# Rotary embedding, fp32: from bf16 passes on ScalarE and VectorE to fp32 in place in a ring, with GpSimd and VectorE computing

## The chip, the cores and the metric

One core of one Trainium2 chip. The metric is the device time of one execution in microseconds (us), median of several executions. "Span" is the time from the first to the last recorded instruction or transfer of the profiled execution; here a time is its span plus 1.7 to 2.2 us. All runs below were in the fast state, with a granted clock of 1.0.

## The reference, cut to what matters

```python
x: [16, 512, 1024] fp32;  cos, sin: [512, 32] fp32;  16 heads of 64
x1, x2 = x[..., :32], x[..., 32:]              # halves of each head
out = concat([x1*cos - x2*sin, x1*sin + x2*cos], axis=-1)   # fp32, [16, 512, 16, 64]
```

The kernel reads 33.5 MB and writes 33.5 MB and does six operations per pair of elements. In the kernel before, the transfers occupy the DMA engines for 98% of the span (below).

## The kernel before

A tile is one batch entry: 4 rows of DRAM (16 KB) to each of 128 partitions, 2 MB. The last two tiles are split into halves and quarters. ScalarE converts a tile to bf16, VectorE does four bf16 operations, ScalarE converts the result back to fp32 and issues the store.

```python
# SyncE: loads, three buffers deep
sp.wait_ge(sem_ci, t - NX + 1)
sp.dma_start(x_sb[:, xb, 0:E], x_tile_ap(t)).then_inc(sem_in[xb], 16)
# ... cut: tables, loaded behind the first tile ...
# ScalarE
ae.activation(xb_sb[:, cb, 0:E], x_sb[:, xb, 0:E], ACT_COPY)          # fp32 -> bf16
ae.activation(o_sb[:, ob, 0:Eu], ob_sb[:, obb, 0:Eu], ACT_COPY)       # bf16 -> fp32
ae.dma_start(out_tile_ap(u), o_sb[:, ob, 0:Eu])
# VectorE, all bf16
ve.tensor_tensor(t1v, xbv, cos_b, mult)
ve.tensor_tensor(t2v, xbv, sin_b, mult)
ve.tensor_tensor(obv[:, :, 0:HALF], t1[:, :, 0:HALF], t2[:, :, HALF:HD], subtract)
ve.tensor_tensor(obv[:, :, HALF:HD], t2[:, :, 0:HALF], t1[:, :, HALF:HD], add)
```

Of the kernel before, what the change touches and what calls it, by code (L numbers as in the profile page):

```python
# [1 line left out]

# [4 lines left out]
def bass_split_heads_rope_kernel(  # L8
    nc: bass.Bass,
    x: bass.AP,  # L10
    cos: bass.AP,
    sin: bass.AP,
    num_heads: bass.AP,
    out: bass.AP,
):
    batch, seq, dim = x.shape
    H = int(num_heads)
    HD = dim // H
    HALF = HD // 2
    P = 128  # L20
    assert seq % P == 0
    SPP = seq // P

    tiles = [(b, 0, SPP) for b in range(batch)]

    def _split(tile, parts):
        b, j0, nj = tile
        if nj % parts != 0:
            return [tile]
        q = nj // parts  # L30
        return [(b, j0 + i * q, q) for i in range(parts)]

    if len(tiles) >= 2:
        t_last = tiles.pop()
        t_prev = tiles.pop()
        tiles += _split(t_prev, 2) + _split(t_last, 4)
    NT = len(tiles)

    ROWS = SPP * H
    RE = ROWS * HD  # L40

    NX = 3
    NC = 3
    NO = 3
    NOB = 3
    NTMP = 2

    fp32 = mybir.dt.float32
    bf16 = mybir.dt.bfloat16
    mult = mybir.AluOpType.mult  # L50
    add = mybir.AluOpType.add
    subtract = mybir.AluOpType.subtract
    ACT_COPY = mybir.ActivationFunctionType.Copy

    with ExitStack() as stack:  # L55
        cos_sb = stack.enter_context(nc.sbuf_tensor([P, SPP, HALF], fp32))
        sin_sb = stack.enter_context(nc.sbuf_tensor([P, SPP, HALF], fp32))
        coscat_sb = stack.enter_context(nc.sbuf_tensor([P, SPP, HD], bf16))
        sincat_sb = stack.enter_context(nc.sbuf_tensor([P, SPP, HD], bf16))
        x_sb = stack.enter_context(nc.sbuf_tensor([P, NX, RE], fp32))  # L60
        xb_sb = stack.enter_context(nc.sbuf_tensor([P, NC, RE], bf16))
        o_sb = stack.enter_context(nc.sbuf_tensor([P, NO, RE], fp32))
        ob_sb = stack.enter_context(nc.sbuf_tensor([P, NOB, RE], bf16))
        tmp1_sb = stack.enter_context(nc.sbuf_tensor([P, NTMP, ROWS, HD], bf16))
        tmp2_sb = stack.enter_context(nc.sbuf_tensor([P, NTMP, ROWS, HD], bf16))
        sem_tab = stack.enter_context(nc.semaphore("sem_tab"))
        sem_tab2 = stack.enter_context(nc.semaphore("sem_tab2"))
        sem_in = [stack.enter_context(nc.semaphore(f"sem_in{i}")) for i in range(NX)]
        sem_out = [stack.enter_context(nc.semaphore(f"sem_out{i}")) for i in range(NO)]
        sem_ci = stack.enter_context(nc.semaphore("sem_ci"))  # L70
        sem_co = stack.enter_context(nc.semaphore("sem_co"))
        sem_vp = stack.enter_context(nc.semaphore("sem_vp"))
        sem_vf = stack.enter_context(nc.semaphore("sem_vf"))
        block = stack.enter_context(nc.Block(no_gpsimd_drain=False))

        cos_v = cos.rearrange("(p j) d -> p (j d)", p=P)
        sin_v = sin.rearrange("(p j) d -> p (j d)", p=P)

        def x_tile_ap(t):
            b, j0, nj = tiles[t]  # L80
            v = x[b, :, :].rearrange("(p j) d -> p j d", p=P)
            return v[:, j0:j0 + nj, :].rearrange("p j d -> p (j d)")

        def out_tile_ap(t):
            b, j0, nj = tiles[t]
            v = out[b, :, :, :].rearrange("(p j) h d -> p j (h d)", p=P)
            return v[:, j0:j0 + nj, :].rearrange("p j e -> p (j e)")

        def uses(nbuf, b):
            return (NT - b + nbuf - 1) // nbuf  # L90

        @block.sync
        def _(sp):
            for t in range(NT):
                xb = t % NX
                _, _, nj = tiles[t]
                E = nj * H * HD
                if t >= NX:
                    sp.wait_ge(sem_ci, t - NX + 1)
                sp.dma_start(x_sb[:, xb, 0:E], x_tile_ap(t)).then_inc(sem_in[xb], 16)  # L100
                if t == 0:
                    sp.dma_start(  # L102
                        cos_sb[:].rearrange("p j d -> p (j d)"), cos_v
                    ).then_inc(sem_tab, 16)
                    sp.dma_start(
                        sin_sb[:].rearrange("p j d -> p (j d)"), sin_v
                    ).then_inc(sem_tab, 16)

        @block.scalar
        def _(ae):  # L110
            ae.wait_ge(sem_tab, 32)
            last = ae.activation(coscat_sb[:, :, 0:HALF], cos_sb[:, :, :], ACT_COPY)  # L112
            last = ae.activation(coscat_sb[:, :, HALF:HD], cos_sb[:, :, :], ACT_COPY)  # L113
            last = ae.activation(sincat_sb[:, :, 0:HALF], sin_sb[:, :, :], ACT_COPY)  # L114
            last = ae.activation(sincat_sb[:, :, HALF:HD], sin_sb[:, :, :], ACT_COPY)  # L115
            last.then_inc(sem_tab2, 1)

            LEAD = 2
            for it in range(NT + LEAD):
                u = it - LEAD  # L120
                if u >= 0:
                    ob = u % NO
                    obb = u % NOB
                    _, _, nju = tiles[u]
                    Eu = nju * H * HD
                    ae.wait_ge(sem_vf, u + 1)
                    if u >= NO:
                        ae.wait_ge(sem_out[ob], 16 * (u // NO))
                    ae.activation(  # L129
                        o_sb[:, ob, 0:Eu], ob_sb[:, obb, 0:Eu], ACT_COPY  # L130
                    ).then_inc(sem_co, 1)
                    ae.wait_ge(sem_co, u + 1)
                    ae.dma_start(out_tile_ap(u), o_sb[:, ob, 0:Eu]).then_inc(sem_out[ob], 16)  # L133
                t = it
                if t < NT:
                    xb = t % NX
                    cb = t % NC
                    _, _, nj = tiles[t]
                    E = nj * H * HD
                    ae.wait_ge(sem_in[xb], 16 * (t // NX + 1))  # L140
                    if t >= NC:
                        ae.wait_ge(sem_vp, t - NC + 1)
                    ae.activation(  # L143
                        xb_sb[:, cb, 0:E], x_sb[:, xb, 0:E], ACT_COPY
                    ).then_inc(sem_ci, 1)
            for b in range(NO):
                ae.wait_ge(sem_out[b], 16 * uses(NO, b))

        @block.vector
        def _(ve):  # L150
            for t in range(NT):
                bt, j0, nj = tiles[t]
                R = nj * H
                E = R * HD
                cb = t % NC
                tb = t % NTMP
                obb = t % NOB
                if t == 0:
                    ve.wait_ge(sem_tab2, 1)
                ve.wait_ge(sem_ci, t + 1)  # L160
                if t >= NTMP:
                    ve.wait_ge(sem_vf, t - NTMP + 1)
                xbv = xb_sb[:, cb, 0:E].rearrange("p (j h d) -> p j h d", j=nj, h=H)
                t1 = tmp1_sb[:, tb, 0:R, :]
                t2 = tmp2_sb[:, tb, 0:R, :]
                t1v = t1.rearrange("p (j h) d -> p j h d", j=nj)
                t2v = t2.rearrange("p (j h) d -> p j h d", j=nj)
                cos_b = coscat_sb[:, j0:j0 + nj, None, :].broadcast_to([P, nj, H, HD])
                sin_b = sincat_sb[:, j0:j0 + nj, None, :].broadcast_to([P, nj, H, HD])
                ve.tensor_tensor(t1v, xbv, cos_b, mult)  # L170
                ve.tensor_tensor(t2v, xbv, sin_b, mult).then_inc(sem_vp, 1)  # L171
                ve.wait_ge(sem_vp, t + 1)
                if t >= NOB:
                    ve.wait_ge(sem_co, t - NOB + 1)
                obv = ob_sb[:, obb, 0:E].rearrange("p (r d) -> p r d", d=HD)
                ve.tensor_tensor(  # L176
                    obv[:, :, 0:HALF], t1[:, :, 0:HALF], t2[:, :, HALF:HD], subtract
                )
                ve.tensor_tensor(  # L179
                    obv[:, :, HALF:HD], t2[:, :, 0:HALF], t1[:, :, HALF:HD], add  # L180
                ).then_inc(sem_vf, 1)


# [1 line left out]
_INS = ['x', 'cos', 'sin', 'num_heads']  # L185
_OUTS = [((16, 512, 16, 64), 'float32')]
#: Inputs that are plain numbers.
_NUMBERS = {'num_heads': 16}


# [24 lines left out]
```

## Time and profile before

163.83 us (median of 3, 163.76 to 163.84), span 162.1 us.

The page of the kernel before, parts 1 to 5, cut. In part 1 a number is busy time, its share of the span, and the count of instructions. In part 2 each digit is the busy share of one fortieth of the span, in tenths. In part 5 the first pair of numbers is total busy us and mean ns of one instruction, and after the bar stands the idle time in front of them, with what ended it. DVE is VectorE, ACT is ScalarE, POOL is GpSimd; a q after a name stands for that engine's sequencer, which issues and waits. The last line is a group of DMA issues, with the size of each and the median us from issue to landing.

```profile
span 162.1 us, 266 instructions
DVE 111.3 (69%) x80; ACT 118.6 (73%) x45; POOL 0.2 (0%) x4
DMA  5999999999999999999999999999999999999985
q1 hardware_dynamic: 3168, 33.69, 49.5%
q10 hardware_dynamic: 2880, 33.56, 48.6%
...
DMA 54%; ACT 30%; issue 7%; DVE 5%; ACTq 1%; SPq 0%; DVEq 0%
...
L143 ACT ACTIVATE xb_sb<-x_sb 128x4096 bf16<-128x4096 f32 (+2 forms) x20 | 58.7, 2933 | 19.9 <-DMA x_sb<-in_x_dram 17.1
L170 DVE TENSOR_TENSOR tmp_sb<-xb_sb,coscat_sb 128x4096 bf16<-128x4096 bf16 (+2 forms) x20 | 37.3, 1865 | 45.8 <-ACT xb_sb L143 45.8
...
out_dram<-o_sb ACTq DMA_DIRECT2D x4, 512.0 KB, 3.6
```

The two transfer queues (q1 loads, q10 stores) occupy the 16 DMA engines for 98% of the span, and the row of 9s has no hole. The compute engines have a quarter to spare. The table by windows gives the same with numbers; its columns are the stretch and its length, busy time and count of VectorE, ScalarE and GpSimd, the TensorE clock, the DMA share and GB/s.

```profile
20.00:40.00 20.00, 18.27 (x11) 18.18 (x6) 0.00 (x0) 1.00 1.01 425
120.00:140.00 20.00, 14.37 (x13) 15.95 (x6) 0.00 (x0) 1.00 1.02 432
155.00:158.00 3.00, 2.05 (x4) 1.84 (x3) 0.00 (x0) 1.00 0.85 345
158.00:160.00 2.00, 0.00 (x0) 0.91 (x1) 0.00 (x0) 1.00 0.54 217
160.00:162.10 2.10, 0.00 (x0) 0.00 (x0) 0.00 (x0) 1.00 0.50 205
```

So 425 to 432 GB/s is what the transfers reach in this kernel when nothing holds them up, and only the ends lose time.

### The profile page before, as it was taken

To read this page: it belongs to the slowest core of one execution; us is meant where nothing else is said; L and a number is where in the kernel's file an instruction comes from. 1 tells how busy PE (TensorE), PEld (TensorE's weight loads), DVE (VectorE), ACT (ScalarE), POOL (GpSimd) and SP (SyncE) were. 2 spreads that over 40 slices of the span, in tenths; PEclk is the share of its full clock that TensorE was granted. 3 is DMA by queue.
4 is the path that set the end of the run, shared out by engine and by line. 5 is a ranking of instruction groups with operands and counts; after the bars stand their busy time and mean duration, and the time that the engine had idled before them with its cause. 6 is when DMAs were issued, how large, how long until landed. Compare 5 with 4: busy or idle time off the path is not lost.

```text
span 162.1 us, 266 instructions
## 1 busy us (share of the span) xinstructions
DVE 111.3 (69%) x80; ACT 118.6 (73%) x45; POOL 0.2 (0%) x4
## 2 busy tenths in 40 slices
DVE  0006997989898989896939488492966994635450
ACT  3078389898989898967588775868859787445552
POOL 0000000000000000000000000000000000000000
DMA  5999999999999999999999999999999999999985
GB/s 158 417 429 449 421 421 412 429 437 421 437 437 425 433 437 421 437 437 425 433 437 417 441 437 414 441 437 417 441 417 427 437 421 444 436 409 423 426 360 212
DMA packets 6050, 67.26 MB, mean 415 GB/s; under 512 B 672, under 2 KB 928, under 8 KB 1952
## 3 DMA queue, kind: packets, MB, share of 16 engines
q1 hardware_dynamic: 3168, 33.69, 49.5%
q10 hardware_dynamic: 2880, 33.56, 48.6%
q14 instruction: 2, 0.02, 0.0%
HBM read 33.69 MB, written 33.55 MB: 415 GB/s over the span
## 4 chain that ended last, share of the span: by engine, by line
DMA 54%; ACT 30%; issue 7%; DVE 5%; ACTq 1%; SPq 0%; DVEq 0%
DMA x_sb<-in_x_dram 49%; ACT xb_sb L143 15%; ACT o_sb L129 14%; DMA sin_sb<-in_sin_dram 5%; DVE tmp_sb L171 2%; DVE tmp_sb L170 1%; ACTq L133 1%; DVE ob_sb L176 1%; DVE ob_sb L179 1%; SPq L102 0%; SPq L100 0%; DVEq L55 0%; ACT coscat_sb L112 0%; ACT sincat_sb L115 0%; ACT coscat_sb L113 0%
## 5 line engine op out<-in xcount | busy, mean ns | idle before, releaser
L143 ACT ACTIVATE xb_sb<-x_sb 128x4096 bf16<-128x4096 f32 (+2 forms) x20 | 58.7, 2933 | 19.9 <-DMA x_sb<-in_x_dram 17.1
L170 DVE TENSOR_TENSOR tmp_sb<-xb_sb,coscat_sb 128x4096 bf16<-128x4096 bf16 (+2 forms) x20 | 37.3, 1865 | 45.8 <-ACT xb_sb L143 45.8
L129 ACT ACTIVATE o_sb<-ob_sb 128x4096 f32<-128x4096 bf16 (+2 forms) x20 | 58.6, 2929 | 12.7 <-DMA out_dram<-o_sb 7.5
L171 DVE TENSOR_TENSOR tmp_sb<-xb_sb,sincat_sb 128x4096 bf16<-128x4096 bf16 (+2 forms) x20 | 37.1, 1857 | 0.0
L176 DVE TENSOR_TENSOR ob_sb<-tmp_sb 128x2048 bf16<-128x2048 bf16 (+2 forms) x20 | 20.2, 1011 | 0.7
L179 DVE TENSOR_TENSOR ob_sb<-tmp_sb 128x2048 bf16<-128x2048 bf16 (+2 forms) x20 | 20.1, 1004 | 0.0
L112 ACT ACTIVATE coscat_sb<-cos_sb 128x128 bf16<-128x128 f32 x1 | 0.3, 309 | 7.0 <-DMA sin_sb<-in_sin_dram 7.0
L112 ACT ACT_TABLE_LOAD x1 | 1.3, 1283 | 0.7 <-PEq L197 0.7
L113 ACT ACTIVATE coscat_sb<-cos_sb 128x128 bf16<-128x128 f32 x1 | 0.3, 293 | 0.0
L115 ACT ACTIVATE sincat_sb<-sin_sb 128x128 bf16<-128x128 f32 x1 | 0.3, 293 | 0.0
L114 ACT ACTIVATE sincat_sb<-sin_sb 128x128 bf16<-128x128 f32 x1 | 0.3, 292 | 0.0
L197 POOL MEMSET const-bfloat16-1.0<- 128x1 bf16 x1 | 0.1, 101 | 0.0
L197 POOL MEMSET const-uint8-127<- 128x1 uint8 x1 | 0.1, 101 | 0.0
L197 POOL MEMSET const-float32-0.0<- 128x1 f32 x1 | 0.1, 98 | 0.2 <-issue 0.2
L197 POOL MEMSET const-float32-1.0<- 128x1 f32 x1 | 0.1, 98 | 0.0
## 6 DMA issues: line engine op xcount, KB each, us to landing
x_sb<-in_x_dram SPq DMA_DIRECT2D x14, 2048.0 KB, 16.8
out_dram<-o_sb ACTq DMA_DIRECT2D x14, 2048.0 KB, 19.7
x_sb<-in_x_dram SPq DMA_DIRECT2D x2, 1024.0 KB, 21.9
x_sb<-in_x_dram SPq DMA_DIRECT2D x4, 512.0 KB, 16.0
out_dram<-o_sb ACTq DMA_DIRECT2D x2, 1024.0 KB, 12.4
out_dram<-o_sb ACTq DMA_DIRECT2D x4, 512.0 KB, 3.6
cos_sb<-in_cos_dram SPq DMA_DIRECT2D x1, 64.0 KB, 7.3
sin_sb<-in_sin_dram SPq DMA_DIRECT2D x1, 64.0 KB, 7.3
```

The costliest lines, as they stand in the source:

```text
L112: last = ae.activation(coscat_sb[:, :, 0:HALF], cos_sb[:, :, :], ACT_COPY)
L113: last = ae.activation(coscat_sb[:, :, HALF:HD], cos_sb[:, :, :], ACT_COPY)
L114: last = ae.activation(sincat_sb[:, :, 0:HALF], sin_sb[:, :, :], ACT_COPY)
L115: last = ae.activation(sincat_sb[:, :, HALF:HD], sin_sb[:, :, :], ACT_COPY)
L129: ae.activation(o_sb[:, ob, 0:Eu], ob_sb[:, obb, 0:Eu], ACT_COPY).then_inc(sem_co, 1)
L133: ae.dma_start(out_tile_ap(u), o_sb[:, ob, 0:Eu]).then_inc(sem_out[ob], 16)
L143: ae.activation(xb_sb[:, cb, 0:E], x_sb[:, xb, 0:E], ACT_COPY).then_inc(sem_ci, 1)
L170: ve.tensor_tensor(t1v, xbv, cos_b, mult)
L171: ve.tensor_tensor(t2v, xbv, sin_b, mult).then_inc(sem_vp, 1)
L176: ve.tensor_tensor(obv[:, :, 0:HALF], t1[:, :, 0:HALF], t2[:, :, HALF:HD], subtract)
L179: ve.tensor_tensor(obv[:, :, HALF:HD], t2[:, :, 0:HALF], t1[:, :, HALF:HD], add).then_inc(sem_vf, 1)
L197: nc = _bacc.Bacc("TRN2", target_bir_lowering=False, num_devices=1)
```

## The change

The intent: no conversions and full fp32, larger contiguous pieces in DRAM (8 rows, 32 KB, where it was 16 KB; such a piece is called a descriptor below, and shows as one packet in the trace), a ring of 40 row slots in SBUF in which x is overwritten by the result, and a share of the work on GpSimd, which was idle. A unit is one row of 1024 elements on each of 128 partitions (512 KB); there are 64 units. For each unit GpSimd makes the sine products (two operations of 512 elements), VectorE the cosine products (one of 1024) and the sum (one of 1024). The cosine table and products lie in PSUM (the other on-chip memory that the program uses), so that each VectorE operation reads one SBUF operand only. The tables are loaded once to 32 partitions and copied on chip to all four groups of 32 partitions (quadrants).

```diff
-    NX = 3; NC = 3; NO = 3; NOB = 3; NTMP = 2
+    R = 16
+    sizes = [[1, 1, 2, 4, 8]] + [[8, 8]] * (G - 2) + [[8, 4, 2, 1, 1]]   # rows of a chunk
+    RING = 40
+    NT1 = 3; NT2 = 4
 ...
+            # SyncE: waits for the store that frees the slots, then
+                sp.dma_start(xs[:, slot:slot + n, :], xv[g, :, r:r + n, :]).then_inc(sem_in[c], 16)
 ...
+            # ScalarE: table loads (cos, then sin), copies of sin to four quadrants, then the stores
+            for c, (g, r, n, slot, at) in enumerate(chunks):
+                ae.wait_ge(sem_v, at + n)
+                ae.dma_start(ov[g, :, r:r + n, :], xs[:, slot:slot + n, :]).then_inc(sem_out[c], 16)
 ...
+        @block.gpsimd
+                if u >= NT2:
+                    pl.wait_ge(sem_v, u - NT2 + 1)
+                for t in range(2):
+                    ins = pl.tensor_tensor(t2_sb[:, u % NT2, :, t, :], x_sb[:, k, :, 1 - t, :],
+                        s_sb[:, r, None, t, :].broadcast_to([P, H, HALF]), mult)
 ...
+        @block.vector
+            def mul(u):      # waits for the chunk and for comb(u - NT1)
+                ve.tensor_tensor(t1_ps[:, u % NT1, :, :], x_sb[:, k, ...], c_ps[:, r, None, :]..., mult)
+            def comb(u):     # waits for mul(u) and GpSimd's unit u
+                ve.tensor_tensor(x_sb[:, k, ...], t1_ps[:, u % NT1, :, :], t2_sb[:, u % NT2, ...], add)
+            LEAD = 2
+            for u in range(NU + LEAD):
+                if u < NU:
+                    mul(u)
+                if u >= LEAD:
+                    comb(u - LEAD)
```

(Lines joined and cut; the ScalarE conversions, the bf16 buffers and the four VectorE operations of before are gone.)

More of the change, by code (lines that the diff above doesn't have):

```diff
@@ L20, in bass_split_heads_rope_kernel @@
     P = 128
-    assert seq % P == 0
-    SPP = seq // P
-    tiles = [(b, 0, SPP) for b in range(batch)]
-    def _split(tile, parts):
-        b, j0, nj = tile
-        if nj % parts != 0:
-            return [tile]
-        q = nj // parts
-        return [(b, j0 + i * q, q) for i in range(parts)]
-    if len(tiles) >= 2:
-        t_last = tiles.pop()
-        t_prev = tiles.pop()
-        tiles += _split(t_prev, 2) + _split(t_last, 4)
-    NT = len(tiles)
-    ROWS = SPP * H
-    RE = ROWS * HD
@@ L42, in bass_split_heads_rope_kernel @@
-    NX = 3
-    NC = 3
-    NO = 3
-    NOB = 3
-    NTMP = 2
+    R = 16
+    SB = seq // R
+    BL = P // SB
+    G = batch // BL
+    assert SB * R == seq and BL * SB == P and G * BL == batch and SB == 32
     fp32 = mybir.dt.float32
-    bf16 = mybir.dt.bfloat16
     mult = mybir.AluOpType.mult
     add = mybir.AluOpType.add
-    subtract = mybir.AluOpType.subtract
-    ACT_COPY = mybir.ActivationFunctionType.Copy
-    with ExitStack() as stack:
-        cos_sb = stack.enter_context(nc.sbuf_tensor([P, SPP, HALF], fp32))
-        sin_sb = stack.enter_context(nc.sbuf_tensor([P, SPP, HALF], fp32))
-        coscat_sb = stack.enter_context(nc.sbuf_tensor([P, SPP, HD], bf16))
-        sincat_sb = stack.enter_context(nc.sbuf_tensor([P, SPP, HD], bf16))
-        x_sb = stack.enter_context(nc.sbuf_tensor([P, NX, RE], fp32))
-        xb_sb = stack.enter_context(nc.sbuf_tensor([P, NC, RE], bf16))
-        o_sb = stack.enter_context(nc.sbuf_tensor([P, NO, RE], fp32))
-        ob_sb = stack.enter_context(nc.sbuf_tensor([P, NOB, RE], bf16))
-        tmp1_sb = stack.enter_context(nc.sbuf_tensor([P, NTMP, ROWS, HD], bf16))
-        tmp2_sb = stack.enter_context(nc.sbuf_tensor([P, NTMP, ROWS, HD], bf16))
-        sem_tab = stack.enter_context(nc.semaphore("sem_tab"))
-        sem_tab2 = stack.enter_context(nc.semaphore("sem_tab2"))
-        sem_in = [stack.enter_context(nc.semaphore(f"sem_in{i}")) for i in range(NX)]
-        sem_out = [stack.enter_context(nc.semaphore(f"sem_out{i}")) for i in range(NO)]
-        sem_ci = stack.enter_context(nc.semaphore("sem_ci"))
-        sem_co = stack.enter_context(nc.semaphore("sem_co"))
-        sem_vp = stack.enter_context(nc.semaphore("sem_vp"))
-        sem_vf = stack.enter_context(nc.semaphore("sem_vf"))
-        block = stack.enter_context(nc.Block(no_gpsimd_drain=False))
-        cos_v = cos.rearrange("(p j) d -> p (j d)", p=P)
-        sin_v = sin.rearrange("(p j) d -> p (j d)", p=P)
-        def x_tile_ap(t):
-            b, j0, nj = tiles[t]
-            v = x[b, :, :].rearrange("(p j) d -> p j d", p=P)
-            return v[:, j0:j0 + nj, :].rearrange("p j d -> p (j d)")
-        def out_tile_ap(t):
-            b, j0, nj = tiles[t]
-            v = out[b, :, :, :].rearrange("(p j) h d -> p j (h d)", p=P)
-            return v[:, j0:j0 + nj, :].rearrange("p j e -> p (j e)")
-        def uses(nbuf, b):
-            return (NT - b + nbuf - 1) // nbuf
@@ new lines, in bass_split_heads_rope_kernel @@
+    COPY = mybir.ActivationFunctionType.Copy
+    sizes = [[1, 1, 2, 4, 8]] + [[8, 8]] * (G - 2) + [[8, 4, 2, 1, 1]]
+    RING = 40
+    chunks = []
+    at = 0
+    for g, ss in enumerate(sizes):
+        r = 0
+        for n in ss:
+            slot = at % RING
+            assert slot + n <= RING
+            chunks.append((g, r, n, slot, at))
+            r += n
+            at += n
+        assert r == R
+    NC = len(chunks)
+    NU = at
+    unit_chunk = []
+    for c, (_, _, n, _, _) in enumerate(chunks):
+        unit_chunk += [c] * n
@@ new lines, in bass_split_heads_rope_kernel @@
+    NT1 = 3
+    NT2 = 4
+    with ExitStack() as stack:
+        x_sb = stack.enter_context(nc.sbuf_tensor([P, RING, H, 2, HALF], fp32))
+        t2_sb = stack.enter_context(nc.sbuf_tensor([P, NT2, H, 2, HALF], fp32))
+        stage = stack.enter_context(nc.sbuf_tensor([SB, 2, R * HALF], fp32))
+        s_sb = stack.enter_context(nc.sbuf_tensor([P, R, 2, HALF], fp32))
+        c_ps = stack.enter_context(nc.psum_tensor([P, R, HALF], fp32))
+        t1_ps = stack.enter_context(nc.psum_tensor([P, NT1, 2 * H, HALF], fp32))
+        sem_in = [stack.enter_context(nc.semaphore(f"in{c}")) for c in range(NC)]
+        sem_out = [stack.enter_context(nc.semaphore(f"out{c}")) for c in range(NC)]
+        sem_cos = stack.enter_context(nc.semaphore("cos"))
+        sem_sin = stack.enter_context(nc.semaphore("sin"))
+        sem_c = stack.enter_context(nc.semaphore("ctab"))
+        sem_s = stack.enter_context(nc.semaphore("stab"))
+        sem_p = stack.enter_context(nc.semaphore("pool"))
+        sem_m = stack.enter_context(nc.semaphore("mul"))
+        sem_v = stack.enter_context(nc.semaphore("comb"))
+        block = stack.enter_context(nc.Block(no_gpsimd_drain=False))
+        xv = x.rearrange("(g b) (s r) d -> g (b s) r d", b=BL, r=R)
+        ov = out.rearrange("(g b) (s r) h d -> g (b s) r (h d)", b=BL, r=R)
+        xs = x_sb[:].rearrange("p n h t d -> p n (h t d)")
@@ L92, in _ @@
         @block.sync
         def _(sp):
-            for t in range(NT):
-                xb = t % NX
-                _, _, nj = tiles[t]
-                E = nj * H * HD
-                if t >= NX:
-                    sp.wait_ge(sem_ci, t - NX + 1)
-                sp.dma_start(x_sb[:, xb, 0:E], x_tile_ap(t)).then_inc(sem_in[xb], 16)
-                if t == 0:
-                    sp.dma_start(
-                        cos_sb[:].rearrange("p j d -> p (j d)"), cos_v
-                    ).then_inc(sem_tab, 16)
-                    sp.dma_start(
-                        sin_sb[:].rearrange("p j d -> p (j d)"), sin_v
-                    ).then_inc(sem_tab, 16)
+            for c, (g, r, n, slot, at) in enumerate(chunks):
+                for e, (_, _, m, eslot, eat) in enumerate(chunks):
+                    if eat < at and eat + RING >= at and eslot < slot + n and slot < eslot + m:
+                        if eat + RING < at + n and eat + m + RING > at:
+                            sp.wait_ge(sem_out[e], 16)
+                sp.dma_start(xs[:, slot:slot + n, :], xv[g, :, r:r + n, :]).then_inc(sem_in[c], 16)
@@ L109, in _ @@
         @block.scalar
         def _(ae):
-            ae.wait_ge(sem_tab, 32)
-            last = ae.activation(coscat_sb[:, :, 0:HALF], cos_sb[:, :, :], ACT_COPY)
-            last = ae.activation(coscat_sb[:, :, HALF:HD], cos_sb[:, :, :], ACT_COPY)
-            last = ae.activation(sincat_sb[:, :, 0:HALF], sin_sb[:, :, :], ACT_COPY)
-            last = ae.activation(sincat_sb[:, :, HALF:HD], sin_sb[:, :, :], ACT_COPY)
-            last.then_inc(sem_tab2, 1)
-            LEAD = 2
-            for it in range(NT + LEAD):
-                u = it - LEAD
-                if u >= 0:
-                    ob = u % NO
-                    obb = u % NOB
-                    _, _, nju = tiles[u]
-                    Eu = nju * H * HD
-                    ae.wait_ge(sem_vf, u + 1)
-                    if u >= NO:
-                        ae.wait_ge(sem_out[ob], 16 * (u // NO))
-                    ae.activation(
-                        o_sb[:, ob, 0:Eu], ob_sb[:, obb, 0:Eu], ACT_COPY
-                    ).then_inc(sem_co, 1)
-                    ae.wait_ge(sem_co, u + 1)
-                    ae.dma_start(out_tile_ap(u), o_sb[:, ob, 0:Eu]).then_inc(sem_out[ob], 16)
-                t = it
-                if t < NT:
-                    xb = t % NX
-                    cb = t % NC
-                    _, _, nj = tiles[t]
-                    E = nj * H * HD
-                    ae.wait_ge(sem_in[xb], 16 * (t // NX + 1))
-                    if t >= NC:
-                        ae.wait_ge(sem_vp, t - NC + 1)
-                    ae.activation(
-                        xb_sb[:, cb, 0:E], x_sb[:, xb, 0:E], ACT_COPY
-                    ).then_inc(sem_ci, 1)
@@ L146, in _ @@
-            for b in range(NO):
-                ae.wait_ge(sem_out[b], 16 * uses(NO, b))
+            ae.dma_start(stage[:, 0, :], cos.rearrange("(s r) d -> s (r d)", r=R)).then_inc(sem_cos, 16)
+            ae.dma_start(stage[:, 1, :], sin.rearrange("(s r) d -> s (r d)", r=R)).then_inc(sem_sin, 16)
+            ae.wait_ge(sem_sin, 16)
+            sv = stage[:, 1, :].rearrange("s (r d) -> s r d", d=HALF)
+            for lo, hi in ((0, 4), (4, R)):
+                for q in range(BL):
+                    ps = slice(q * SB, (q + 1) * SB)
+                    ae.activation(s_sb[ps, lo:hi, 0, :], sv[:, lo:hi, :], COPY, scale=-1.0)
+                    ae.activation(s_sb[ps, lo:hi, 1, :], sv[:, lo:hi, :], COPY).then_inc(sem_s, 1)
@@ new lines, in _ @@
+            for c, (g, r, n, slot, at) in enumerate(chunks):
+                ae.wait_ge(sem_v, at + n)
+                ae.dma_start(ov[g, :, r:r + n, :], xs[:, slot:slot + n, :]).then_inc(sem_out[c], 16)
+            for c in range(NC):
+                ae.wait_ge(sem_out[c], 16)
+        @block.gpsimd
+        def _(pl):
+            for u in range(NU):
+                c = unit_chunk[u]
+                g, r0, n, slot, at = chunks[c]
+                r = r0 + u - at
+                k = slot + u - at
+                if u == at:
+                    pl.wait_ge(sem_in[c], 16)
+                if u == 0:
+                    pl.wait_ge(sem_s, BL)
+                if r == 4 and g == 0:
+                    pl.wait_ge(sem_s, 2 * BL)
+                if u >= NT2:
+                    pl.wait_ge(sem_v, u - NT2 + 1)
+                for t in range(2):
+                    ins = pl.tensor_tensor(
+                        t2_sb[:, u % NT2, :, t, :],
+                        x_sb[:, k, :, 1 - t, :],
+                        s_sb[:, r, None, t, :].broadcast_to([P, H, HALF]),
+                        mult,
+                    )
+                ins.then_inc(sem_p, 1)
@@ L149, in _ @@
         @block.vector
         def _(ve):
-            for t in range(NT):
-                bt, j0, nj = tiles[t]
-                R = nj * H
-                E = R * HD
-                cb = t % NC
-                tb = t % NTMP
-                obb = t % NOB
-                if t == 0:
-                    ve.wait_ge(sem_tab2, 1)
-                ve.wait_ge(sem_ci, t + 1)
-                if t >= NTMP:
-                    ve.wait_ge(sem_vf, t - NTMP + 1)
-                xbv = xb_sb[:, cb, 0:E].rearrange("p (j h d) -> p j h d", j=nj, h=H)
-                t1 = tmp1_sb[:, tb, 0:R, :]
-                t2 = tmp2_sb[:, tb, 0:R, :]
-                t1v = t1.rearrange("p (j h) d -> p j h d", j=nj)
-                t2v = t2.rearrange("p (j h) d -> p j h d", j=nj)
-                cos_b = coscat_sb[:, j0:j0 + nj, None, :].broadcast_to([P, nj, H, HD])
-                sin_b = sincat_sb[:, j0:j0 + nj, None, :].broadcast_to([P, nj, H, HD])
-                ve.tensor_tensor(t1v, xbv, cos_b, mult)
-                ve.tensor_tensor(t2v, xbv, sin_b, mult).then_inc(sem_vp, 1)
-                ve.wait_ge(sem_vp, t + 1)
-                if t >= NOB:
-                    ve.wait_ge(sem_co, t - NOB + 1)
-                obv = ob_sb[:, obb, 0:E].rearrange("p (r d) -> p r d", d=HD)
-                ve.tensor_tensor(
-                    obv[:, :, 0:HALF], t1[:, :, 0:HALF], t2[:, :, HALF:HD], subtract
-                )
-                ve.tensor_tensor(
-                    obv[:, :, HALF:HD], t2[:, :, 0:HALF], t1[:, :, HALF:HD], add
-                ).then_inc(sem_vf, 1)
@@ new lines, in _ @@
+            ve.wait_ge(sem_cos, 16)
+            cv = stage[:, 0, :].rearrange("s (r d) -> s r d", d=HALF)
+            for q in range(BL):
+                ins = ve.tensor_copy(c_ps[q * SB:(q + 1) * SB, :, :], cv)
+            ins.then_inc(sem_c, 1)
+            ve.wait_ge(sem_c, 1)
+            def mul(u):
+                c = unit_chunk[u]
+                g, r0, n, slot, at = chunks[c]
+                r = r0 + u - at
+                k = slot + u - at
+                if u == at:
+                    ve.wait_ge(sem_in[c], 16)
+                if u >= NT1:
+                    ve.wait_ge(sem_v, u - NT1 + 1)
+                ve.tensor_tensor(
+                    t1_ps[:, u % NT1, :, :],
+                    x_sb[:, k, :, :, :].rearrange("p h t d -> p (h t) d"),
+                    c_ps[:, r, None, :].broadcast_to([P, 2 * H, HALF]),
+                    mult,
+                ).then_inc(sem_m, 1)
@@ new lines, in comb @@
+            def comb(u):
+                c = unit_chunk[u]
+                g, r0, n, slot, at = chunks[c]
+                k = slot + u - at
+                ve.wait_ge(sem_m, u + 1)
+                ve.wait_ge(sem_p, u + 1)
+                ve.tensor_tensor(
+                    x_sb[:, k, :, :, :].rearrange("p h t d -> p (h t) d"),
+                    t1_ps[:, u % NT1, :, :],
+                    t2_sb[:, u % NT2, :, :, :].rearrange("p h t d -> p (h t) d"),
+                    add,
+                ).then_inc(sem_v, 1)
```

## The prediction

> **What bounds the kernel now.** The 16 DMA engines. The page gives the queues 49.5% + 48.6% of the span of 162.1 us; the table by windows shows a DMA share of 0.98 to 1.05 from 4 to 155 us (about 430 GB/s). ScalarE (118.6 us busy) and VectorE (111.3) have a quarter to spare. The loss is at the ends: nothing moves before 1.7 us, and in the last 7 us the share falls to 0.85, 0.54, 0.50. The time (163.8) is the span plus 1.7.
>
> **What DMA can still give.** In the trace's packet records a 4 KB packet takes 159 ns, 8 KB 309, 16 KB 611: some 302 ns per 8 KB plus 8 ns. So 32 KB should take 1.22 us, which saves half a per cent. Packets now sum to 157.4 us per engine; after, I add up 156.6 (48 of 64 units in 32 KB packets, the rest in 4 to 16 KB). With the same ends, a DMA-bound version has a span near 160.5: 1% better.
>
> **What is removed, added, moved.** ScalarE's 40 conversions (117 us) and the bf16 VectorE work go. A unit is now 128x1024 fp32 (2.44 us of DMA for both ways); there are 64.
> - VectorE does two fp32 operations of 1024 elements per unit. [...] 2048 elements take 1.22 us, or 1.14 start to start when chained[...]. With three product buffers each multiply waits for the combine just ahead of it, so only one of the two is chained: 1.14 + 1.22 + 0.04 = 2.40 us[...]. I take 2.45.
> - GpSimd does two of 512 elements. [...] VectorE reads one SBUF operand per instruction[...].
>
> **Start.** The multiply of unit u precedes the combine of u-2 on VectorE, and the multiply of unit 8 needs chunk 4 (8 rows at once). Before it each DMA engine has loads of 19.6 us and early stores of 5 us: it lands at about 27.5 us. Combines 0 to 5 are done by about 22 us, so VectorE and GpSimd wait some 5 us. Then loads run ahead and DMA no longer limits.
>
> **Sum.** The last combine ends at 27.5 + 58 x 2.45 = 169.6; the last store takes 3.1 us from issue, as before: span 172.8, time **174 us**, range 164 to 185. Faster by over 2%: 0.05; within 2%: 0.2; slower: 0.75.
>
> **What would show it.** Chain of waits: mostly VectorE (or GpSimd), DMA only in the first 28 us. VectorE over 85% busy; DMA share about 0.9 or less, spread over the span. A VectorE wait of about 5 us on a load near 22 us. VectorE operations of 1.2 us[...]. Packets of 32 KB of about 1.22 us.
>
> **What would make it wrong.** If a unit costs 2.3 us or less on both engines, or the first stall is absent, the kernel stays DMA-bound at about 162. [...]

Where cuts are marked above, passages are taken out that no trace had shown: on fp32 against bf16 on VectorE, on GpSimd's times, and on operands in PSUM and SBUF. The 1.22 and 1.14 us are those of the bf16 operations of 2048 elements in the kernel before; that VectorE's fp32 operations of 1024 elements take as long was the assumption. The sum came to what it says, 27.5 + 58 x 2.45 + 3.1 = 172.8 us of span and 174 us of time: its 2.45 is the 2.40 of that assumption and a margin, and GpSimd had no term of its own in it.

## The result, and the profile after

170.24 us (4 runs, 169.93 to 170.63), against 163.84 us for the kernel before (163.76 to 164.05). The ratio is 1.0373, 95% interval 1.0334 to 1.0411: slower by 3.7%. The ratio and its interval are taken from fast runs of the same rounds; it is not quite the ratio of the medians quoted here.

The page of the changed kernel, the lines that answer to those above:

```profile
span 168.3 us, 434 instructions
DVE 154.8 (92%) x132; ACT 7.1 (4%) x17; POOL 155.7 (92%) x132
DMA  5999999999999999999999999999999992289895
q1 hardware_dynamic: 2016, 33.56, 47.5%
q10 hardware_dynamic: 2112, 33.69, 47.0%
...
POOL 86%; issue 6%; DMA 3%; POOLq 1%; ACT 1%; DVE 1%; ACTq 0%; DVEq 0%
...
L121 POOL TENSOR_TENSOR t_sb<-x_sb,s_sb 128x512 f32<-128x512 f32 x128 | 155.5, 1311 | 7.9 <-ACT s_sb L98 7.9
L147 DVE TENSOR_TENSOR t_ps<-x_sb,c_ps 128x1024 f32<-128x1024 f32 x64 | 78.5, 1229 | 3.4 <-DMA x_sb<-in_x_dram 0.6
L160 DVE TENSOR_TENSOR x_sb<-t_ps,t_sb 128x1024 f32<-128x1024 f32 x64 | 78.2, 1221 | 2.5 <-POOL t_sb L121 2.5
...
out_dram<-x_sb ACTq DMA_DIRECT2D x4, 512.0 KB, 9.4
```

The chain of waits has turned from DMA to GpSimd. GpSimd waits 7.9 us for its table and then never again: 155.5 us of busy time without a gap, while its last instruction ends at 163.9 us. VectorE is as full by its share, and the profile alone does not say which of the two sets the pace. The DMA row now has a hole, at 141 to 146 us:

```profile
120.00:140.00 20.00, 19.66 (x18) 0.00 (x0) 20.00 (x18) 1.00 1.00 427
140.00:150.00 10.00, 9.79 (x9) 0.00 (x0) 10.00 (x9) 1.00 0.40 170
150.00:155.00 5.00, 4.86 (x5) 0.00 (x0) 5.00 (x5) 1.00 0.99 421
```

The way to read this: the transfers run at full rate until 139 us although they do not set the end, because the ring lets loads run ahead (the last loads are issued at 101 us). By 142 us all 64 units are loaded and 48 stored (the last load lands at 142.2 us, that store at 141.3); 112 units at 1.22 us is 137 us of transfers. After that only stores are left, and these come at the pace of compute: one unit, 1.22 us of transfer, per 2.43 us. A full DMA row for five sixths of the span therefore did not mean that DMA was the limit.

The timeline near 22 us and at the end (start, length, engine, line, operation, shapes, count, and in brackets the idle time ahead of it with what ended it):

```profile
23.08 1.23 DVE L160 TENSOR_TENSOR x_sb<-t_ps,t_sb 128x1024 f32<-128x1024 f32 x1
24.95 1.23 DVE L147 TENSOR_TENSOR t_ps<-x_sb,c_ps 128x1024 f32<-128x1024 f32 x1 [0.64 <-DMA x_sb<-in_x_dram]
...
159.22 1.22 DVE L160 TENSOR_TENSOR x_sb<-t_ps,t_sb 128x1024 f32<-128x1024 f32 x1
160.47 5.11 ACTq L101 DMA_DIRECT2D out_dram<-x_sb  x3
161.55 1.23 DVE L160 TENSOR_TENSOR x_sb<-t_ps,t_sb 128x1024 f32<-128x1024 f32 x1 [1.12 <-POOL t_sb L121]
163.98 1.23 DVE L160 TENSOR_TENSOR x_sb<-t_ps,t_sb 128x1024 f32<-128x1024 f32 x1 [1.21 <-POOL t_sb L121]
```

The wait for the fifth load is 0.64 us, where I had predicted some 5. The chain of waits gives GpSimd's true spacing, here 16 instructions at a time:

```profile
22.94 18.76 POOL t_sb L121 x16
41.70 0.67 issue
42.36 1.27 POOL t_sb L121
```

From 22.94 to 42.36 is 19.42 us for 16 instructions: 1.214 us each, 2.43 us per unit. The mean length on the page, 1311 ns, is longer than that, and cannot be the pace: 128 x 1.311 would be 168 us, more than the 155.5 us in which they all ran. So GpSimd is timed here by start-to-start spacing, not by the recorded length.

### The profile page after: what moved, and what is told of

It reads as the page before. It is cut to its first block, busy times and chain, and to the rows that moved or that the text cites. A ratio compares the mean times of both kernels' runs of the same rounds, so it can differ in the third digit from the quotient of the medians.

```text
span 168.3 us, 434 instructions
## 1 busy us (share of the span) xinstructions
DVE 154.8 (92%) x132; ACT 7.1 (4%) x17; POOL 155.7 (92%) x132
## 4 chain that ended last, share of the span: by engine, by line
POOL 86%; issue 6%; DMA 3%; POOLq 1%; ACT 1%; DVE 1%; ACTq 0%; DVEq 0%
POOL t_sb L121 86%; DMA stage<-in_sin_dram 3%; POOLq L57 1%; ACT s_sb L97 1%; DVE x_sb L160 1%; ACT s_sb L98 0%; ACTq L90 0%; DVEq L159 0%; POOLq L115 0%
## 5 line engine op out<-in xcount | busy, mean ns | idle before, releaser
L121 POOL TENSOR_TENSOR t_sb<-x_sb,s_sb 128x512 f32<-128x512 f32 x128 | 155.5, 1311 | 7.9 <-ACT s_sb L98 7.9
L147 DVE TENSOR_TENSOR t_ps<-x_sb,c_ps 128x1024 f32<-128x1024 f32 x64 | 78.5, 1229 | 3.4 <-DMA x_sb<-in_x_dram 0.6
L160 DVE TENSOR_TENSOR x_sb<-t_ps,t_sb 128x1024 f32<-128x1024 f32 x64 | 78.2, 1221 | 2.5 <-POOL t_sb L121 2.5
L134 DVE COPY c_ps<-stage 32x512 f32<-32x512 f32 x4 | 2.8, 689 | 4.5 <-DMA stage<-in_cos_dram 4.5
L97 ACT ACTIVATE s_sb<-stage 32x128 f32<-32x128 f32 (+1 forms) x8 | 3.3, 415 | 3.4 <-DMA stage<-in_sin_dram 3.2
L98 ACT ACTIVATE s_sb<-stage 32x128 f32<-32x128 f32 (+1 forms) x8 | 3.2, 398 | 0.0
```

The lines of the kernel that those rows point to most:

```text
L97: ae.activation(s_sb[ps, lo:hi, 0, :], sv[:, lo:hi, :], COPY, scale=-1.0)
L98: ae.activation(s_sb[ps, lo:hi, 1, :], sv[:, lo:hi, :], COPY).then_inc(sem_s, 1)
L121: ins = pl.tensor_tensor(t2_sb[:, u % NT2, :, t, :], x_sb[:, k, :, 1 - t, :], s_sb[:, r, None, t, :].broadcast_to([P, H, HALF]), mult,)
L134: ins = ve.tensor_copy(c_ps[q * SB:(q + 1) * SB, :, :], cv)
L147: ve.tensor_tensor(t1_ps[:, u % NT1, :, :], x_sb[:, k, :, :, :].rearrange("p h t d -> p (h t) d"), c_ps[:, r, None, :].broadcast_to([P, 2 ...
L160: ve.tensor_tensor(x_sb[:, k, :, :, :].rearrange("p h t d -> p (h t) d"), t1_ps[:, u % NT1, :, :], t2_sb[:, u % NT2, :, :, :].rearrange("p ...
```

## The experiments

The theories. **G**: GpSimd's pace of 2.43 us per unit sets the time. **V**: VectorE's pace, 2.39 to 2.43 us per unit, sets it. **D**: the new layout of transfers does (chunks of 8 rows, loads that run ahead, the hole). The predictions of these theories for each run are quoted, less the passages whose cut is marked. In all, 12 kernels ran, each against the kernel before on the same chip in 3 or 5 rounds; its medians there were 163.77 to 163.89 us.

### lead1: VectorE with no wait on its own previous instruction

```diff
-            LEAD = 2
+            LEAD = 1
```

> Only the lead of VectorE's multiply over its combine goes from 2 units to 1, so that no VectorE instruction waits for the one just ahead of it; results stay right. Theory G (GpSimd's 128 multiplies at 1.216 us start to start set the pace): VectorE's pair falls from 2.39 to about 2.28 us and its idle time grows by that much, but the time stays at 170.2 +- 0.6 us, GpSimd without a gap. Theory V (VectorE's 2.39 to 2.43 us per unit set the pace): 64 x 0.11 = 7 us less, about 163 to 164 us. Theory D (the layout of the transfers: chunks of 8 units, loads that run ahead): no change.

Measured: 169.95 us (ratio 1.0377 [1.0342, 1.0412]), correct. Two lines of its page:

```profile
L121 POOL TENSOR_TENSOR t_sb<-x_sb,s_sb 128x512 f32<-128x512 f32 x128 | 155.2, 1252 | 7.8 <-ACT s_sb L98 7.8
L160 DVE TENSOR_TENSOR x_sb<-t_ps,t_sb 128x1024 f32<-128x1024 f32 x64 | 78.4, 1225 | 6.4 <-POOL t_sb L121 2.4
```

The time is that of the changed kernel, and GpSimd has no gap. VectorE is faster when left alone (2.26 us per unit, seen below in the run with both edits), but here its combines still come 2.42 us apart, at GpSimd's pace. V falls. The expected growth of VectorE's idle time by 7 us does not show: in front of its multiplies and combines the pages have 5.9 us before and 6.4 us now. In the changed kernel a combine starts 1.14 us after the multiply just ahead of it, which is recorded as 1.23 us, so most of the slack lies inside the recorded lengths.

### vec_half: half the multiply on VectorE (wrong result)

```diff
-                    t1_ps[:, u % NT1, :, :],
-                    x_sb[:, k, :, :, :]...,  c_ps[:, r, None, :].broadcast_to([P, 2 * H, HALF])
+                    t1_ps[:, u % NT1, 0:H, :],
+                    x_sb[:, k, 0:H // 2, :, :]..., c_ps[:, r, None, :].broadcast_to([P, H, HALF])
# the combine reads that half twice
```

> VectorE's multiply covers half the elements (512 instead of 1024) and the combine reads that half twice (wrong result on purpose), so VectorE needs about 1.85 us per unit; GpSimd's work and the transfers are unchanged. G: 170 +- 1 us, GpSimd's spacing stays 1.216 us. V: DMA-bound, about 162 to 163. D: 170. If the two engines disturb each other, GpSimd's spacing falls below 1.2 us and the time by some us.

Measured: 170.29 us (1.0385 [1.0359, 1.041]). Three lines of its page:

```profile
DVE 125.6 (75%) x132; ACT 7.1 (4%) x17; POOL 155.6 (92%) x132
L121 POOL TENSOR_TENSOR t_sb<-x_sb,s_sb 128x512 f32<-128x512 f32 x128 | 155.4, 1251 | 8.0 <-ACT s_sb L98 8.0
L160 DVE TENSOR_TENSOR x_sb<-t_ps,t_sb 128x1024 f32<-128x1024 f32 x64 | 78.4, 1225 | 31.1 <-POOL t_sb L121 31.0
```

VectorE's busy time fell by 29 us (from 154.8) and nothing was gained; VectorE's combines now wait 31 us for GpSimd. GpSimd's busy total is the same 155.4 us, so the half of the multiply that was taken away had not been slowing it either.

### pool_half: half the work on GpSimd (wrong result)

```diff
-                for t in range(2):
+                for t in range(1):
# the combine reads that half twice
```

> GpSimd does one of its two multiplies per unit and the combine reads that half twice (wrong result on purpose); VectorE's work and the transfers are as in the changed kernel. G: GpSimd is no longer the pace, VectorE's 2.39 us per unit is next: the first combine comes 1.2 us earlier and 63 units save 0.03 to 0.04 us each, so about 3 us less, 167 +- 1 us. V: only the earlier first combine, about 169. D: 170. [...]

Measured: 168.87 us (1.0301 [1.0279, 1.0324]); the expectation of G, 167 +- 1, was too large a gain. GpSimd is off the path: it waits 62.0 us for VectorE's combines. VectorE alone then runs at 2.40 us per unit against 2.42 with full GpSimd work, so nearly the same limit stood right behind the first. The last combine ended 3.7 us earlier (161.55 against 165.21), but the time fell only 1.4 us, and the timeline shows why:

```profile
156.93 1.23 DVE L147 TENSOR_TENSOR t_ps<-x_sb,c_ps 128x1024 f32<-128x1024 f32 x1
158.07 3.48 DVE L160 TENSOR_TENSOR x_sb<-t_ps,t_sb 128x1024 f32<-128x1024 f32 x3
159.32 2.77 ACTq L101 DMA_DIRECT2D out_dram<-x_sb  x3
```

The last three combines (units 61 to 63) come back to back here, 1.13 us apart, and the transfers of the four units that they release need 1.23 us each at the 425 GB/s of the kernel before. From the start of unit 61's combine to the end of the span it is 9.0 us here and 9.1 us in the changed kernel (159.22 to 168.3). So unit 61 counts for the end, not unit 63, when the last ones bunch up. Unit 61 came 1.15 us earlier.

### lead1_pool_half: both engines relieved (wrong result)

The edit is that of lead1 and that of pool_half together:

```diff
-            LEAD = 2
+            LEAD = 1
-                for t in range(2):
+                for t in range(1):
```

> Both edits: lead 1, and one GpSimd multiply per unit (wrong result on purpose). GpSimd needs 1.22 us and VectorE about 2.28 us per unit, both below the 2.44 us of DMA. G and V: the kernel becomes DMA-bound, span near 161, 162 to 164 us, the hole in the transfers at 140 to 148 us gone. D: stays at 168 or more, because the transfers themselves are slow.

Measured: 164.56 us (1.0032 [1.0001, 1.0063]). The table by windows:

```profile
4.00:140.00 136.00, 134.97 (x121) 5.77 (x16) 76.11 (x61) 1.00 1.01 429
140.00:150.00 10.00, 9.48 (x9) 0.00 (x0) 2.51 (x2) 1.00 0.96 412
150.00:158.00 8.00, 3.49 (x3) 0.00 (x0) 1.25 (x1) 1.00 0.99 419
```

Full transfers to 158 us, no hole. The units are combined every 2.26 us until 149 us; then VectorE waits 2.8 us, and GpSimd 8.3, for a load that ends the wait at 152 us. The kernel is bound by transfers again, at the time of the kernel before and not below it. (The chain of waits on its page still names VectorE for 43% and DMA for 14%; the reading rests on the DMA share of 0.96 to 1.01 in the table.) D falls: these same transfers, in the same chunks, lose no more than 0.3% once compute keeps up. It also bounds the change: with compute out of the way it would have won nothing here.

### l1ph_16k: the same with descriptors of at most 16 KB (wrong result)

```diff
-    sizes = [[1, 1, 2, 4, 8]] + [[8, 8]] * (G - 2) + [[8, 4, 2, 1, 1]]
+    sizes = [[1, 1, 2, 4, 4, 4]] + [[4, 4, 4, 4]] * (G - 2) + [[4, 4, 4, 2, 1, 1]]
```

> The transfer-bound variant (lead 1, half of GpSimd's work, wrong result on purpose; 164.6 us) with chunks of at most 4 rows, so descriptors of at most 16 KB as in the kernel before. By packet times (1213 ns for 32 KB, 611 for 16 KB) the larger descriptors are worth (2 x 611 - 1213) x 96 packets = 0.9 us: 165.4 if only that counts. Rival: chunk size counts by what it makes wait (8 units must be combined before a store starts, 8 must land before work starts), then smaller chunks are as fast or faster, 162 to 164.6.

Measured: 164.17 us (1.0021 [1.0006, 1.0037]), against 164.56 us with 32 KB (another chip, so compare the ratios: 1.0021 and 1.0032, intervals that overlap). The 0.9 us is not seen in the time, and the packet records tell why: the 0.9 us was computed from medians. The median of a 32 KB packet is 1213 ns, as expected, but some take up to 2.4 us (2.5 in the changed kernel), and the mean in lead1_pool_half is 1225 ns, which is two 16 KB packets of this run at their mean of 613. All packets together take 49.1% + 48.7% of 162.6 us there and 49.2% + 48.9% of 162.0 us here, 159.0 and 158.9 us. The larger descriptors, a stated aim of the change, saved no transfer time at all.

### after_16k: the changed kernel with smaller chunks

The same edit of the chunk sizes, on the changed kernel alone.

> The changed kernel with chunks of at most 4 rows (descriptors of at most 16 KB); results right. In the changed kernel the transfers stand still from 141 to 146 us, because the store of units 48 to 55 waits for its eighth unit. If that gap costs time by itself (theory D), smaller chunks win 3 us or more, 167 or less. G: GpSimd still works without a gap from 8.4 us and the last combine still ends at about 165.2, and the last store already lands 2.6 us after issue, so the gap is only a sign of slow compute: 170.2 +- 0.6 us.

Measured: 170.46 us (1.0401 [1.0387, 1.0415]), correct. As G expected. The size of chunks is not the cause.

### t1_sbuf: the cosine products in SBUF instead of PSUM

```diff
-        t1_ps = stack.enter_context(nc.psum_tensor([P, NT1, 2 * H, HALF], fp32))
+        t1_ps = stack.enter_context(nc.sbuf_tensor([P, NT1, 2 * H, HALF], fp32))
```

> The changed kernel with the cosine products kept in SBUF instead of PSUM, so that VectorE's combine reads two SBUF operands; results stay right. [...] a unit costs GpSimd's 2.43 plus up to the combine's 1.22 us: between 2.43 and 3.65 us, a time of up to 248 us, with GpSimd's or VectorE's operations stretched or gaps before them. If there is no such sharing, 170.2 +- 1 us, and the PSUM detour bought nothing.

Measured: 231.99 us (1.4157 [1.4134, 1.4181]), correct. Its groups by form:

```profile
L121 POOL TENSOR_TENSOR t_sb<-x_sb,s_sb 128x512 f32<-128x512 f32 x128 | 217.3, 1738 | 8.0 <-ACT s_sb L98 8.0
L160 DVE TENSOR_TENSOR x_sb<-t_ps,t_sb 128x1024 f32<-128x1024 f32 x64 | 139.0, 2171 | 2.9 <-POOL t_sb L121 2.9
L147 DVE TENSOR_TENSOR t_ps<-x_sb,c_ps 128x1024 f32<-128x1024 f32 x64 | 78.0, 1221 | 2.9
```

The combine, which now reads two SBUF operands, takes 2.17 us instead of 1.22; the multiply, which still reads one, keeps 1.22. GpSimd's starts alternate between 1.21 and 2.20 us. A unit takes 3.41 us. So with two SBUF operands the combine, and one of the two GpSimd operations of a unit, took 0.95 and 0.99 us longer; the trace does not show by what mechanism. With the combine and GpSimd's operations not overlapped at all, a unit would take 2.43 + 1.22 = 3.65 us; the measured 3.41 is 0.24 less, and no run here shows why. The detour through PSUM was worth 62 us, and the changed kernel shows no such stretching: its combine takes 1.22 us and GpSimd keeps its 1.21 us.

### sin_first: GpSimd's table first

```diff
-            ae.dma_start(stage[:, 0, :], cos...)
-            ae.dma_start(stage[:, 1, :], sin...)
+            ae.dma_start(stage[:, 1, :], sin...)
+            ae.dma_start(stage[:, 0, :], cos...)
```

> The changed kernel with its two table loads swapped: sin, for which GpSimd waits, goes out first, cos second; results stay right. In the changed kernel cos, issued first, landed at 4.45 us and sin at 6.11. G (time = GpSimd's start 8.4 + 64 x 2.43 + 4.4): GpSimd starts at about 6.7 us and the time falls by the same 1.6 us, to 168.6 +- 0.6. If something later in the chain (the fifth load at 25 us, the transfers) decides, the time stays at 170.2.

Measured: 169.7 us (1.0359 [1.0343, 1.0376]), correct. A miss: 0.5 us instead of 1.6. GpSimd did start at 6.60 instead of 8.38 us. But VectorE waits for cos, which now lands second:

```profile
8.86 3.49 DVE L147 TENSOR_TENSOR t_ps<-x_sb,c_ps 128x1024 f32<-128x1024 f32 x3
...
12.26 1.22 DVE L160 TENSOR_TENSOR x_sb<-t_ps,t_sb 128x1024 f32<-128x1024 f32 x1
```

Its first combine is at 12.26 us; in the changed kernel it was at 10.94. At 2.40 us per unit VectorE hardly makes this up. The page's chain of waits still names GpSimd (88%), because the last combine waits for it, but as in pool_half the end goes with the combine of unit 61, which is on VectorE's pace: it starts at 158.81 us where it started at 159.22, only 0.4 us earlier, and 9.0 us before the end of the span.

### sin_first_16k: sin first with smaller chunks

The edit of sin_first and that of l1ph_16k (chunks of at most 4 rows) together.

> Sin first and chunks of at most 4 rows; results right. With sin first alone the last combine came 2.0 us earlier but the time fell only 0.5 us, and the last store landed 4.0 us after issue instead of 2.6. My explanation: the store of 8 units is issued at 145.5 us and 16 units of stores then keep DMA full to the end. If so, smaller chunks let these stores start earlier and free the rest of the gain: 168.3 +- 0.5 us. If the explanation is wrong, it stays at 169.7.

Measured: 169.8 us (1.0363 [1.0347, 1.038]), correct. Not 168.3: my first explanation of the miss, that a store of 8 units at 145.5 us blocks the end, was wrong. (In its profiled run the tables also came about 0.7 us later.) It was then that I saw VectorE's late start, which the next run tests.

### lead1_sin_first: sin first, and a VectorE that can catch up

The edit of sin_first and that of lead1 together.

> Sin first together with lead 1; results right. Sin first alone let GpSimd start 1.8 us earlier but VectorE, which waits for cos, began its first combine 1.3 us later (12.26 instead of 10.94 us), and at 2.39 to 2.40 us per unit it had no slack to catch up. With lead 1 VectorE needs 2.27 us per unit and catches up within some 20 units. G: GpSimd again works without a gap, from about 6.6 us to 161.9, and its start counts one to one: 168.4 +- 0.5 us. Rival, the transfers at the end decide: it stays at 169.5 or above.

Measured: 168.96 us (1.0314 [1.0299, 1.0328]), correct. In the profiled run GpSimd started at 6.97 us, 1.4 us earlier than in the changed kernel, and its last instruction ended at 162.13, 1.75 earlier; the span is 166.6 us, 1.7 shorter. The median is 1.3 us lower and lies 0.06 us above the interval that I had given, with GpSimd's start 0.4 us later than expected; the profiled run was the fastest of the five. The cleaner comparison is with lead1, from which only the order of the tables differs: GpSimd starts 1.3 us earlier (8.28 there) and the ratio falls from 1.0377 to 1.0314, 1.0 us. So GpSimd's start counts in the time nearly in full once VectorE can follow, as G says; that it counts one to one is not shown.

### balanced and balanced_16k: moving some of GpSimd's work to VectorE

Both keep the result right. With lead 1 VectorE has slack, and takes over some units' sine products, with their sine rows in PSUM:

```diff
+    def on_dve(u):                      # sine operations of unit u that VectorE does
+        if u == NU - 1: return 1
+        return 2 if u % R == 7 else 0   # balanced_16k: only for u > R
...
-                for t in range(2):
+                for t in range(2 - on_dve(u)):          # GpSimd
+                for t in range(2 - on_dve(u), 2):       # VectorE, in mul(u)
+                    ve.tensor_tensor(t2_sb[:, u % NT2, :, t, :], x_sb[:, k, :, 1 - t, :], s_ps[...], mult)
```

> Lead 1, sin first, and VectorE takes over the sine products of one unit in 16 and half of those of the last unit, with their sine rows in PSUM; results stay right. GpSimd has 60.5 units of 2.43 = 147 us, VectorE 64 x 2.26 + 4.5 x 1.2 = 150 us, DMA about 156 to 159. G: the loss was GpSimd's surplus alone, so the kernel becomes DMA-bound, as in the variant of 164.6 us or a little better: 163.5 +- 1.2 us, within 1% of the kernel before. If it stays above 167, something other than GpSimd's pace costs time.

Measured: 165.44 us (1.0097 [1.0082, 1.0112]), correct. 4.8 us of the 6.4 us lost came back, 0.7 us less than the interval allowed. VectorE is now the pace, and from its first combine on: the combines are 2.26 us apart from 11.15 us to the end, 1.2 to 1.6 us more at each moved unit. (A late start, as the next expectation has it, is not the reason: in the changed kernel the first combine is at 10.94 us.)

> Lead 1, tables in the order of the change (cos first, which VectorE waits for), chunks of at most 4 rows, and VectorE takes over three units' sine products and half of the last unit's; results right. The version of 165.4 us was paced by VectorE, which began its first combine late and had 9 extra operations. Here VectorE: first combine at about 10.9 us, 63 x 2.26 + 7 x 0.64 + 1.2, the last combine ends near 159, plus 3.1 us of store and 1.8: 164.0 +- 0.8 us, that is the time of the kernel before, since transfers alone allow about 163.8. Under 162.5 would mean that the transfers' bound is lower than I think; over 165.5 that balance is not the cause.

Measured: 167.23 us (1.021 [1.0196, 1.0224], so whether it is 2% slower than the kernel before is left unclear), correct. A miss. In its chain of waits GpSimd leads until 130 us and VectorE from there to the end. My sum had taken each engine's total, but the first taken-over unit is 23, and until then VectorE is held to GpSimd's pace: its combines come 2.43 us apart for 21 units, up to 62 us, and 2.26 apart from there to the end. The 0.17 us of each of these units, 3.4 us in all, cannot be used later. It is not a better balance than the other. No version beat the kernel before, and lead1_pool_half shows about how little was to be had.

## Why the prediction was right or wrong, point by point

The outcome was as predicted in direction, and the time (174, range 164 to 185) is 3.8 us too high.

- **Transfers bound the kernel before, and larger descriptors cannot give 2%**: right. With compute relieved the new transfers take 164.56 us, the old size 164.17, the kernel before 163.8. The median 32 KB packet takes 1213 ns (I had 1.22 us). But the 1% that I gave a DMA-bound version did not come: its span was 162.6 us and not 160.5, and its packets sum to 159.0 us per engine where I had 156.6 from medians (see l1ph_16k).
- **"VectorE operations of 1.2 us"**: right. 1.22 to 1.23 us for 1024 elements in fp32 with one of two operands in PSUM, the same as for 2048 in bf16 with SBUF operands only in the kernel before (1.22). The multiply took 1221 ns with its result in SBUF (t1_sbuf) and 1219 to 1229 with it in PSUM (lead1, the changed kernel); what a read from PSUM costs, no run here singles out.
- **The unchained multiply**: right. 2.40 us per unit with lead 2 (pool_half), 2.26 with lead 1 (lead1_pool_half). In the changed kernel a multiply starts 1.25 us after the combine that it waits for, and a combine 1.14 after the multiply ahead of it.
- **GpSimd's time per unit**: measured as 1.213 us per operation, 2.43 per unit.
- **Which engine**: I put the sum on VectorE at 2.45 us and named GpSimd in brackets. vec_half and lead1 show that it was GpSimd; pool_half shows VectorE 0.02 to 0.03 us per unit behind. Freeing one alone gave at most 1.4 us, freeing both gave 5.7. That a sum along VectorE's path came close is partly luck: the two paces differ by about 1% here, and the 2.45 had a margin on VectorE's own 2.40 that GpSimd's 2.43 happens to fill.
- **The start, "VectorE and GpSimd wait some 5 us" for a load at "about 27.5 us"**: wrong. This is the step that failed. The load came by 24.95 us and the wait was 0.64 us. The term that I mis-sized is "early stores of 5 us" ahead of it. The trace's packet records of the changed kernel, packets started in each us:

```
us   load packets of 32 KB   store packets of 4 KB
16            13                      10
18            15                      13
20            11                      14
22            15                      16
```

  The two queues start about equally many packets (92 and 100 from 16 to 24 us), though a load's had 32 KB and a store's 4 KB. Up to the load's landing only 118 store packets had started, 1.2 us of work per engine instead of 5: not even all 128 of the first unit's store. By what rule the engines choose between the queues is not shown: the trace does not name the engine of a packet. The first store of 512 KB, issued at 12.20 us, started its first packet at 15.67 and took 15.2 us to land, the second 23.7; the two at the end, with no loads beside them, took 3.6 and 2.6. (The page's 9.4 us is the median of these four; the 3.6 us of the kernel before is of stores at the end only.) I had counted all the early stores as done ahead of the load. The other half of that error was that the tables came later than I thought (sin at 6.1 us), so there was less to wait with: VectorE reached the multiply of unit 8 at 24.3 us, not at 22.
- **The sum, term by term**: the multiply of unit 8 at 24.95 instead of 27.5 (-2.55); from there to the end of the last combine 140.3 us for 58 units instead of 142.1 (-1.85, 2.418 per unit and not 2.45); the last store 3.1 us, as predicted. Together 168.3 instead of 172.8. In going from span to time I had added only 1.2 us, where it is 1.9.
- **"If ... the first stall is absent, the kernel stays DMA-bound at about 162"**: wrong, and at odds with my own sum. The stall was all but absent (0.64 us) and the time was 170.24. With combines 0 to 5 done at 22 us, no stall and 58 units of 2.45 us, my terms give a span of 167, not 160: the pace of compute, not the stall, made the kernel slower. The other half of that sentence held: with both engines under 2.3 us per unit (lead1_pool_half) it is DMA-bound, at 164.56.
- **"DMA share about 0.9 or less, spread over the span"**: wrong. It was 1.0 to 139 us and then had a hole, because the loads ran ahead.
- **"VectorE over 85% busy"**: right (92%), though it did not set the pace. **"Chain of waits: mostly VectorE (or GpSimd)"**: it was GpSimd, 86%.

What stays open: why some 32 KB packets take up to 2.4 us, which uses up the 0.7% that the others save.

## What to carry to other kernels

Before moving work to use idle engines in a kernel that transfers bound, add up each engine's time per unit of transfer, start to start and with the waits of its own order: three resources at 2.40 to 2.44 us leave no room for a start of 8.4 us and an end of 4.4. When two engines are within 2% of each other, an experiment on one of them shows little of the gain (1.4 of 5.7 us here); relieve both to see the bound behind them. And a transfer row that is full for most of the span does not prove that transfers are the limit if the buffers let loads run ahead: look at what happens when the loads are over.
